# Where w_out's first half lands, and which engine issues the x tiles, in a pooling and gated-linear-attention block

## The chip, the cores and the metric

The kernel runs on one core of one Trainium2 chip. A core has a matrix engine (TensorE, PE in the profile; PEld is its weight load), a vector engine (VectorE, DVE), a scalar engine (ScalarE, ACT), GpSimd (POOL), and a sequencer (SyncE, SP) that in this kernel issues every transfer between memory and the core. Each engine works through its own list of instructions in order and waits for the others by semaphores. The metric is the device time of one execution in microseconds (us).

## What is computed

One block of a streaming encoder over 1024 rows of width 1024, after 16 meta rows: a mixer and a squared-ReLU MLP, all in float32. Cut to what matters here:

```python
def hybrid_mixer(u, ...):
    a, q, k, v, r, lr, ga, gb = split(u @ w_in)
    y_a = pooled(a) @ w_pool_out
    o = gla_chunked(q, k, v, log_a)                  # the attention, chunk by chunk
    y_b = (rmsnorm(o) * silu(r)) @ w_gla_out
    m = sigmoid(ga) * y_a + sigmoid(gb) * y_b        # the merge
    return m @ w_out
h = h + hybrid_mixer(rmsnorm(h), ...)
h = h + squared_relu_mlp(rmsnorm(h), w_ff1, w_ff2)
return rmsnorm(h)
```

The change sits between the end of `gla_chunked` and the product `m @ w_out`.

## The kernel before

**Split products.** Every float32 operand of a product is used as a high part (a copy rounded to the matrix engine's format, made by ACT) and a low part (the difference, made by DVE or POOL). A product is three matmuls for each 128 rows of depth, in `mm3` (L246 high by high, L247, L248). When the right-hand side is converted late, the first of the three needs only its high part, the second its low part. When the left-hand side is, the third needs its low part.

**Stages around the change.** The sequence is split into two halves of 512 rows. While the attention runs, a list of fill steps gives the matrix engine other work; the last of them are the merge blocks of half 0, `yb_block(n, 0)`. When the last attention unit has been started, `early_gates` runs: it turns on a hand-written order for ACT and DVE (their instructions then stand exactly in the order of the program text, as PE's do throughout), and takes space on the right-hand side of the memory for `t2`, `o2` and `raw3`, over tiles of the attention that are done (`n0`, `n1`, `f`, `y`, `lr`). Then come, in this order of the program: `merge_open`; the four merge blocks of half 1, `yb_block(0..3, 1)`; the conversion of the first half of w_out in four chunks of 512 KB, `load_wo(0, 0..3)`; `wo1_open`, which ends the hand-written order; eight output tiles `out_tile(t, 0)` for the left 512 columns, with the conversion of w_out's other half between them; eight output tiles for the right columns.

**A merge block** is two sub-blocks of 12 matmuls (four steps of depth by three). The text after the prediction's heading calls the blocks of half 1 B0 to B3, and their sub-blocks e0 and e1. DVE empties each sub-block's bank with L1060 (times a gate, `t`) and L1061 (plus the pooled part, `o`), ACT makes the high part (L1064, `th`), POOL the low part (L1065, `tl`). The gates and pooled parts are read back by SP (L1008, L1009) into three buffers each, so a load waits until POOL or DVE has used the buffer three sub-blocks earlier.

**w_gla_out** reaches the blocks through `W1`, a ring of two converted weights: SP loads into a raw tile (`Raw.load`, L101), ACT makes `w1h` (L77), DVE `w1l` (L78). B0 and B1 use weights kept from half 0. The weights of B2 are converted in the middle of B0 and those of B3 in the middle of B1, each between that block's two sub-blocks. Here they are called G2 and G3.

**w_out's chunks**, C0 to C3 here, are loaded into the same raw tiles and converted by ACT (L1345) and DVE (L1346). In the program text C0 stands behind B1, C1 behind B2, C2 and C3 behind B3. An output tile takes the four chunks one after the other, six matmuls each, and adds the x tile in L1378. The x tile was loaded into the same `acc` tile by SP (L1337, `x_again`), whose first tiles lie over buffers of the merge blocks of half 0.

**Banks.** Merge blocks and output tiles take turns over four banks of the matrix engine's result memory (`mm`, `mm`, `x`, `x`). Output tile 0 takes the bank that B2e0 had, so it cannot start before DVE has emptied that one.

**SP and POOL** are not in the hand-written order. The planner of the framework orders their instructions by its own estimate of when each becomes ready, and each then executes its list in that order.

Of the kernel before, what the change touches and what calls it, by code (L numbers as in the profile page):

```python
# [15 lines left out]
P = 128  # L16
D = 1024
# [3 lines left out]
HALF = 512  # L21
# [84 lines left out]
def kernel(  # L106
# [3 lines left out]
    nc = tc.nc  # L110
    x = x[0]
    out = out[0]
    norm_mix, w_in, w_pool_mix, pool_scale, w_pool_out = norm_mix[0], w_in[0], w_pool_mix[0], pool_scale[0], w_pool_out[0]
    w_gate_up, b_gate, gla_norm, w_gla_out, w_out = w_gate_up[0], b_gate[0], gla_norm[0], w_gla_out[0], w_out[0]
    norm_ffn, w_ff1, w_ff2 = norm_ffn[0], w_ff1[0], w_ff2[0]

    act, dve, pool, pe = nc.scalar, nc.vector, nc.gpsimd, nc.tensor
# [6 lines left out]
    def banks(keep=0, **tags):  # L124
        while len(ps_open) > keep:
            ps_open.pop().__exit__(None, None, None)
            wide.pop(psp.popitem()[0], None)
        for tag, n in tags.items():
            cm = tc.tile_pool(name=f"ps_{tag}", bufs=n, space=bass.MemoryType.PSUM)
            psp[tag] = cm.__enter__()  # L130
            ps_open.append(cm)
# [31 lines left out]
    gB = left.push("gB", [P, D], F32)  # L163
# [16 lines left out]
    raw = Raw(nc, [left.push(f"raw{i}", [P, D], F32) for i in range(2)])  # L180
# [10 lines left out]
    def f32(ap):  # L191
        return ap.bitcast(F32)
# [4 lines left out]
    def bcast(v):  # L197
        return v[None, :].broadcast_to([P, D])
# [202 lines left out]
    S, rings = {}, [W1]  # L401

    def step(steps, fn, ring=None, aps=()):
        steps.append((ring, list(aps), fn))
# [393 lines left out]
    one = []  # L798
# [122 lines left out]
    def rows4(w, j):  # L921
        return w[:, j * 256 : (j + 1) * 256].rearrange("(k p) c -> p k c", p=P)
# [79 lines left out]
    def yb_load(n, h):  # L1002

        if n >= 8 or (n, h) in staged:
            return
        d = 2 * YB[h][n // 2] + n % 2
        gl, ml = staged[n, h] = (nxt("t2"), nxt("o2")) if h else (nxt("t1"), nxt("o"))
        nc.sync.dma_start(gl, gb_dram[d, h])  # L1008
        nc.sync.dma_start(ml, ma_dram[d, h])  # L1009

    def in_order(on):


        if on:
            S["order"] = tc.manual_schedule(engines={mybir.EngineType.Activation, mybir.EngineType.DVE})
            S["order"].__enter__()
        else:
            S.pop("order").__exit__(None, None, None)

    def early_gates():  # L1020

        in_order(True)
        left.pop_to(S["left_n"])
        for key in ("t2", "o2"):
            S[key] = right.push(key, [P, 3, HALF], F32)
            S["n" + key], S["d" + key] = 0, 3
        S["raw3"] = right.push("raw3", [P, D], F32)
        for n in range(3):
            yb_load(n, 1)

# [2 lines left out]
    def yb_block(n, h):  # L1033
        j = YB[h][n]

        def fn(*wbs):
            if h == 0 and n > 1:
                kept[j] = wbs[0]
            wb = wbs[0] if wbs else kept[j]
            hi, lo = (t.rearrange("p (k c) -> p k c", k=4) for t in wb)  # L1040
            assert h or ("o", 0) in done
            yg = S["yg"][h]
            for e in range(2):
                d, w = 2 * j + e, slice(e * P, (e + 1) * P)
                for m in range(2 + h):
                    yb_load(2 * n + e + m, h)
                gl, ml = staged[2 * n + e, h]
                b = bank("mm")
                for k in range(4):
                    mm3(  # L1050
                        b, 1, lambda i: (hi[:, k, w], lo[:, k, w]),
                        lambda i: (yg[:, 0, k], yg[:, 1, k]), first=k == 0, last=k == 3,
                    )
                    yield 3 * 512 / 2400
                if e and not wbs:
                    W1.done, W1.kept = W1.done + 1, W1.kept - 1
                    W1.top_up()
                elif e:
                    yield "keep" if j in kept else "free"
                dve.tensor_tensor(gl, b, gl, ALU.mult)  # L1060
                dve.tensor_tensor(gl, gl, ml, ALU.add)  # L1061
                th = MH[h][:, d]
                tl = ML[h][:, d]
                act.activation(th, gl, ACT.Copy)  # L1064
                pool.tensor_tensor(tl, gl, f32(th), ALU.subtract)  # L1065

        return fn
# [216 lines left out]
    def gla():  # L1284
# [16 lines left out]
        for n, u in enumerate(units + [None]):  # L1301
            if u is None:
                early_gates()
            live = side + old + ([inside(*u, units[n - 1] if n else None)] if u else [])
            while live:
                waits = [(g, next(g, None)) for g in live]
                live = [g for g, w in waits if w is not None]
                pour(max([w for _, w in waits if w is not None], default=0) * PACE)
                if not live:
                    break  # L1310
            if n == 2:
                done.add(("o", 0))
            if n == 0:
                while ("k", 1) not in done:
                    next(filler)
            old = [across(*u)] if u else []
            side = [meta_state(1)] if n == 0 else []
# [7 lines left out]
    def merge_open():  # L1325
        W1.eng = dve
        banks(keep=1, x=2, ms=4)
        rota["mm"] = ("mm", "mm", "x", "x")
        left.pop_to(base)
        S["wo"] = [left.push("wo0", [P, 2, KT, HALF], F32R)]  # L1330
        S["left_acc"] = left.mark()
        S["acc"] = left.push("acc", [P, 8, D], F32)
        raw.lend(S["raw3"])
        nc.sync.dma_start(gB, bcast(norm_ffn))

    def x_again(t):
        nc.sync.dma_start(S["acc"][:, t], x[t * P : (t + 1) * P, :])  # L1337

    def load_wo(ch, kk):
        def fn():  # L1340
            wo = S["wo"][ch][:, :, 2 * kk : 2 * kk + 2]
            c = slice(ch * HALF, (ch + 1) * HALF)
            r = raw.load(w_out[kk * 256 : (kk + 1) * 256, c].rearrange("(k p) c -> p k c", p=P), D)
            r = r.rearrange("p (k c) -> p k c", k=2)
            act.activation(wo[:, 0], r, ACT.Copy)  # L1345
            dve.tensor_tensor(wo[:, 1], r, f32(wo[:, 0]), ALU.subtract)  # L1346

        return fn

    step(one, merge_open)  # L1350
    def wo1_open():
        in_order(False)
# [12 lines left out]
    def out_tile(t, ch):  # L1365
        def fn():
            half, at = t // 4, (t % 4) * P
            wo = S["wo"][ch]
            b, n = bank("mm"), ORDER.index(t)
            for j in range(2):  # L1370
                if ch and j and n > 1:
                    turn_tile(ORDER[n - 2])
                mm3(
                    b, KT // 2, lambda i: (MH[half][:, 4 * j + i, at : at + P], ML[half][:, 4 * j + i, at : at + P]),
                    lambda i: (wo[:, 0, 4 * j + i], wo[:, 1, 4 * j + i]), first=j == 0, last=j == 1,
                )
            a = S["acc"][:, t, ch * HALF : (ch + 1) * HALF]
            dve.tensor_tensor(a, b, a, ALU.add)  # L1378
            if ch:
                layer_norm(S["acc"][:, t], S["u2"][:, n % 2])  # L1380
                nc.sync.dma_start(h_dram[t], S["acc"][:, t])

        return fn

    def turn_tile(t, tags=("ms",)):
# [26 lines left out]
        for n, a in enumerate((lo, b12)):  # L1412
            fh, fl = (S["wo"][0][:, k, 4 * n : 4 * n + 4, cols] for k in range(2))
            act.activation(fh, a, ACT.Copy)
            dve.tensor_tensor(fl, a, f32(fh), ALU.subtract)

    for n, j in enumerate(YB[1]):
        if n < 2:
            step(one, yb_block(n, 1))
        else:  # L1420
            step(one, yb_block(n, 1), W1, [rows4(w_gla_out, j)])
        if n:
            step(one, load_wo(0, n - 1))
    step(one, load_wo(0, 3))
    step(one, wo1_open)
    for t in range(8):
        step(one, lambda t=t: x_again(t))
        step(one, out_tile(t, 0))
        if 1 < t < 6:
            step(one, load_wo(1, t - 2))  # L1430
# [268 lines left out]
```

## Time and profile before

| what | value |
|---|---|
| median of three runs | 1243.65 us (1243.61 to 1248.66) |
| the profiled execution | 1241.63 us, its span 1239.6 us |
| TensorE clock granted, mean | 0.996 of full |
| PE busy from 500 to 515 us | 15.00 of 15 us |
| PE busy from 515 to 525 us | 4.76 of 10 us |
| PE busy from 530 to 570 us | 40.00 of 40 us |

A row of the timeline gives the start in us, the length in us, engine, line, operation, the tile written and the tiles read, the number of instructions merged into the row, and in brackets how long the engine had been idle just before and what ended that. A row of the waits gives who waited for what, the total in us, how often, and the longest. A row of the windows gives, for a stretch of time, its length and the busy time of PE, PEld, DVE, ACT and POOL with instruction counts, then the granted clock, the share of the transfer engines' time in use, and GB/s. Successive matmuls of 512 columns start 0.23 us apart at full clock, though each is listed as 0.39 us long, since they are pipelined.

### The profile page before, as it was taken

Reading aid. Unit: us, or ns where it says so; the run is one execution under the profiler, and the core shown is the slowest. Engines: PE = TensorE matmul, PEld = TensorE weight load, DVE = VectorE, ACT = ScalarE, POOL = GpSimd, SP = SyncE. Lnnn points to the kernel's source line nnn. Section 1 sums busy time; section 2 is a strip of 40 time slices with the busy share of each in tenths; the row PEclk is TensorE's granted clock in tenths of the full one; section 3 lists DMA queues with packets and bytes.
Section 4 is the critical chain, followed back from the end, with each engine's and each line's share of the span. In section 5 each row is a group of like instructions: output and inputs, shape, how many; then the busy total and the mean of one; then the engine's idle time right before and its main releaser. Section 6 shows DMA issues by size and latency. Waiting matters only on the chain.

```text
span 1239.6 us, 18265 instructions
## 1 busy us (share of the span) xinstructions
PE 1206.1 (97%) x6816; PEld 1003.1 (81%) x6816; DVE 850.9 (69%) x1388; ACT 618.8 (50%) x1099; POOL 66.6 (5%) x74
## 2 busy tenths in 40 slices
PE   7999999999999999899999999999999999999997
PEld 6878888988887778688878888888887788888886
DVE  6896676654556676634896676776774877887686
ACT  6667567322446663412654454555553444444554
POOL 2100000001101015400000000000000000000000
PEclk9999999999999999899999999999999999999999
DMA  8033326146102247831244444444569863333432
GB/s 250 2 110 104 110 86 193 53 155 219 36 19 78 69 133 234 282 109 51 98 125 159 156 153 143 162 156 134 176 216 374 289 235 102 94 99 98 162 98 89
DMA packets 142680, 173.84 MB, mean 140 GB/s; under 512 B 10968, under 2 KB 82416, under 8 KB 142592
## 3 DMA queue, kind: packets, MB, share of 16 engines
q1 hardware_dynamic: 142592, 172.68, 43.3%
q8 instruction: 53, 0.87, 0.3%
q14 instruction: 35, 0.29, 0.1%
HBM read 119.17 MB, written 53.48 MB: 139 GB/s over the span
## 4 chain that ended last, share of the span: by engine, by line
PE 85%; DVE 8%; ACT 3%; DMA 2%; issue 2%; SPq 0%; DVEq 0%; ACTq 0%
PE b_mm L246 10%; PE b_mm L247 10%; PE b_mm L248 10%; PE b_ms L247 9%; PE b_ms L246 9%; PE b_ms L248 9%; PE b_x L248 8%; PE b_x L246 8%; PE b_x L247 8%; PE b_sc L1147 1%; PE b_ms L550 1%; PE b_mx L246 1%; PE b_m L1249 1%; PE b_mx L247 1%; PE b_mx L248 1%
## 5 line engine op out<-in xcount | busy, mean ns | idle before, releaser
L246 PE MATMUL b_mm<-th,w1h 128*128 128x512 f32 (+1 forms) x312 | 117.6, 377 | 1.9 <-DVE c L761 1.1
L247 PE MATMUL b_mm<-tl,w1h 128*128 128x512 f32 (+1 forms) x312 | 116.0, 372 | 0.6 <-DVE tl L1407 0.6
L248 PE MATMUL b_mm<-th,w1l 128*128 128x512 f32 (+1 forms) x312 | 115.8, 371 | 0.0
L246 PE MATMUL b_x<-th,w1h 128*128 128x512 f32 (+1 forms) x240 | 90.8, 378 | 0.0
L247 PE MATMUL b_x<-tl,w1h 128*128 128x512 f32 (+1 forms) x240 | 90.6, 378 | 0.0
L248 PE MATMUL b_x<-th,w1l 128*128 128x512 f32 (+1 forms) x240 | 90.3, 376 | 0.0
L264 ACT ACTIVATE w1h<-raw 128x512 fp32r<-128x512 f32 x96 | 59.6, 621 | 36.8 <-PE b_x L247 14.1
L265 DVE TENSOR_TENSOR w1l<-raw,w1h 128x512 fp32r<-128x512 f32 x96 | 65.6, 684 | 12.9 <-ACT w1h L264 12.9
L246 PEld LDWEIGHTS b_mm<-th,w1h 128*128 128x128 f32 x312 | 58.6, 188 | 13.7 <-issue 1.8
L264 ACT ACTIVATE w1h<-fs 128x512 fp32r<-128x512 f32 x72 | 45.4, 631 | 45.8 <-PE b_ms L247 31.5
L247 PEld LDWEIGHTS b_mm<-tl,w1h 128*128 128x128 f32 x312 | 58.6, 188 | 10.6 <-DVE tl L1407 0.9
L248 PEld LDWEIGHTS b_mm<-th,w1l 128*128 128x128 f32 x312 | 58.6, 188 | 10.3
L264 ACT ACTIVATE w1h<-bt 128x512 fp32r<-128x512 f32 x44 | 27.8, 632 | 67.7 <-issue 59.6
L265 DVE TENSOR_TENSOR w1l<-fs,w1h 128x512 fp32r<-128x512 f32 x72 | 49.3, 685 | 14.7 <-ACT w1h L264 14.6
L1556 DVE TENSOR_TENSOR bt<-w,w 128x512 f32<-128x512 f32 x80 | 54.6, 683 | 1.0 <-DMA w<-in_w_ff_dram 1.0
L248 PEld LDWEIGHTS b_x<-th,w1l 128*128 128x128 f32 x240 | 45.1, 188 | 8.4
L246 PEld LDWEIGHTS b_x<-th,w1h 128*128 128x128 f32 x240 | 45.0, 188 | 8.5
L247 PEld LDWEIGHTS b_x<-tl,w1h 128*128 128x128 f32 x240 | 45.1, 188 | 8.3
L264 ACT ACTIVATE fxh<-bt 128x512 fp32r<-128x512 f32 x36 | 22.8, 632 | 55.4 <-issue 48.1
L246 PE MATMUL b_ms<-wo,w1h 128*128 128x512 f32 x128 | 49.8, 389 | 0.0
L247 PE MATMUL b_ms<-wo,w1h 128*128 128x512 f32 x128 | 49.8, 389 | 0.0
L248 PE MATMUL b_ms<-wo,w1l 128*128 128x512 f32 x128 | 49.8, 389 | 0.0
(446 smaller groups left out, 3365.2 us busy)
## 6 DMA issues: line engine op xcount, KB each, us to landing
hf_dram<-h SPq DMA_DIRECT2D x112, 256.0 KB, 2.1
raw<-hf_dram SPq DMA_DIRECT2D x112, 256.0 KB, 2.7
w<-in_w_ff_dram SPq DMA_DIRECT2D x64, 256.0 KB, 4.9
raw<-in_w_in_dram SPq DMA_DIRECT2D x24, 512.0 KB, 4.9
raw<-in_w_ff_dram SPq DMA_DIRECT2D x16, 512.0 KB, 4.1
rawx<-in_w_ff_dram SPq DMA_DIRECT2D x16, 512.0 KB, 4.1
xs<-in_x_dram SPq DMA_DIRECT2D x8, 512.0 KB, 4.7
rawx<-in_w_in_dram SPq DMA_DIRECT2D x8, 512.0 KB, 4.7
```

The source lines that it names most:

```text
L246: pe.matmul(ps, ah, bh, start=first and i == 0, stop=False, skip_group_check=more)
L247: pe.matmul(ps, ah, bl, start=False, stop=False, skip_group_check=more)
L248: pe.matmul(ps, al, bh, start=False, stop=last and i == n - 1, skip_group_check=more)
L264: act.activation(hi, a, ACT.Copy)
L265: dve.tensor_tensor(lo, a, f32(hi), ALU.subtract)
L550: pe.transpose(b[j][:, i], u[:, (4 * j + i) * P : (4 * j + i + 1) * P], ident)
L1147: pe.matmul(b[to, e, j], kk[r, s], qq[r, s], start=True, stop=True, tile_position=(e * CH, u * CH))
L1249: pe.matmul(o[part(u), e, j], scc[part(u), e, j], v[part(u), j, e], start=j == 0, stop=False, tile_position=(u * CH, u * CH), skip_group_c ...
L1556: dve.tensor_tensor(bt, w, S["w2"][q[3:]][:, i], ALU.add if q[2] == "+" else ALU.subtract)
```

## The change

C0 is loaded into `raw3` already in `early_gates`, and `raw3` is no longer one of the raw tiles. C1, C2 and C3 are loaded into the last three tiles of `acc` as soon as `merge_open` has made them. The conversions of C0, C1 and C2 move forward by two blocks and that of C3 by one: C0 stands ahead of B0, C1 ahead of B1, C2 ahead of B2, C3 ahead of B3. The x tiles and the row `gB` are issued by ACT in place of SP: tile 0 before B3, tile 1 after B3, tile t + 2 ahead of output tile t. SP is not put into a hand-written order.

```diff
@@ early_gates
         S["raw3"] = right.push("raw3", [P, D], F32)
+        fetch_wo(0, 0, S["raw3"])
         for n in range(3):
             yb_load(n, 1)
@@ merge_open and behind it
         S["acc"] = left.push("acc", [P, 8, D], F32)
-        raw.lend(S["raw3"])
-        nc.sync.dma_start(gB, bcast(norm_ffn))
+        for kk in (1, 2, 3):
+            fetch_wo(0, kk, S["acc"][:, 4 + kk])
+
+    def load_gB():
+        act.dma_start(gB, bcast(norm_ffn))
 
     def x_again(t):
-        nc.sync.dma_start(S["acc"][:, t], x[t * P : (t + 1) * P, :])
+        act.dma_start(S["acc"][:, t], x[t * P : (t + 1) * P, :])
+
+    fetched = {}
+
+    def fetch_wo(ch, kk, at=None):
+
+        c, rows = slice(ch * HALF, (ch + 1) * HALF), w_out[kk * 256 : (kk + 1) * 256]
+        ap = rows[:, c].rearrange("(k p) c -> p k c", p=P)
+        if at is None:
+            at = raw.load(ap, D)
+        else:
+            nc.sync.dma_start(at.rearrange("p (k c) -> p k c", k=2), ap)
+        fetched[ch, kk] = at.rearrange("p (k c) -> p k c", k=2)
 
     def load_wo(ch, kk):
         def fn():
-            wo = S["wo"][ch][:, :, 2 * kk : 2 * kk + 2]
-            c = slice(ch * HALF, (ch + 1) * HALF)
-            r = raw.load(w_out[kk * 256 : (kk + 1) * 256, c].rearrange("(k p) c -> p k c", p=P), D)
-            r = r.rearrange("p (k c) -> p k c", k=2)
+            if (ch, kk) not in fetched:
+                fetch_wo(ch, kk)
+            wo, r = S["wo"][ch][:, :, 2 * kk : 2 * kk + 2], fetched.pop((ch, kk))
             act.activation(wo[:, 0], r, ACT.Copy)
             dve.tensor_tensor(wo[:, 1], r, f32(wo[:, 0]), ALU.subtract)
@@ the list of steps
+    def loads(*ts):
+        def fn():
+            for t in ts:
+                x_again(t)
+
+        return fn
+
     for n, j in enumerate(YB[1]):
+        step(one, load_wo(0, n))
+        if n == 3:
+            step(one, loads(0))
         if n < 2:
             step(one, yb_block(n, 1))
         else:
             step(one, yb_block(n, 1), W1, [rows4(w_gla_out, j)])
-        if n:
-            step(one, load_wo(0, n - 1))
-    step(one, load_wo(0, 3))
+    step(one, loads(1))
     step(one, wo1_open)
+    step(one, lambda: load_gB())
     for t in range(8):
-        step(one, lambda t=t: x_again(t))
+        if t < 6:
+            step(one, loads(t + 2))
         step(one, out_tile(t, 0))
         if 1 < t < 6:
             step(one, load_wo(1, t - 2))
```

## The prediction

> **What bounds the kernel now.** I read the page's first rows, then the matrix engine's waits, longest first, to find a hole that this change could close.
>
> ```profile
> span 1239.6 us, 18265 instructions
> PE 1206.1 (97%) x6816; PEld 1003.1 (81%) x6816; DVE 850.9 (69%) x1388; ACT 618.8 (50%) x1099; POOL 66.6 (5%) x74
> ```
>
> ```profile
> PE b_mm L246 <- ACT wo L1345: 2.8, 1, 2.8
> PE b_mm L247 <- DVE wo L1346: 2.4, 2, 1.4
> ```
>
> PE sets the time: it is busy for 97% of the span. Its two longest waits in the middle of the kernel are both for w_out's chunks. Its timeline shows where.
>
> ```profile
> 513.66 0.39 PE L246 MATMUL b_mm<-wo,th 128*128 128x512 f32 x1
> ...
> 516.99 0.50 PE L247 MATMUL b_mm<-wo,th 128*128 128x512 f32 x1 [1.37 <-DVE wo L1346]
> ...
> 521.25 0.79 PE L246 MATMUL b_mm<-wo,th 128*128 128x512 f32 x1 [2.83 <-ACT wo L1345]
> 523.09 0.80 PE L247 MATMUL b_mm<-wo,th 128*128 128x512 f32 x1 [1.04 <-DVE wo L1346]
> ...
> 527.09 0.39 PE L246 MATMUL b_x<-wo,th 128*128 128x512 f32 x1
> ```
>
> Output tile 0 starts at 513.66 and tile 1 at 527.09: 13.43 us for 24 matmuls. Part of that is a lower clock, as the windows of one microsecond show (the last column but two).
>
> ```profile
> 519.00:520.00 1.00, 0.00 (x0) 0.00 (x0) 0.59 (x1) 0.38 (x1) 1.00 (x1) 0.62 0.85 164
> 520.00:521.00 1.00, 0.00 (x0) 0.00 (x0) 0.00 (x0) 1.00 (x2) 1.00 (x2) 0.50 0.88 225
> ...
> 526.00:527.00 1.00, 1.00 (x6) 0.82 (x5) 1.00 (x2) 0.22 (x1) 0.00 (x0) 0.97 0.97 348
> ```
>
> The pace without a hole is read from the block before it.
>
> ```profile
> 503.24 0.39 PE L248 MATMUL b_mm<-yg,w1l 128*128 128x512 f32 x1
> ...
> 508.22 0.39 PE L246 MATMUL b_x<-yg,w1h 128*128 128x512 f32 x1
> 508.45 0.39 PE L247 MATMUL b_x<-yg,w1h 128*128 128x512 f32 x1
> 508.68 0.39 PE L248 MATMUL b_x<-yg,w1l 128*128 128x512 f32 x1
> ```
>
> B3 runs from 508.22 to 513.66: 24 matmuls in 5.44 us, or 0.227 each. So the hole costs 13.43 - 5.44 = 7.99 us. That is all the change can win: PE is full from 530 to 570.
>
> Why the chunks are late is read from DVE, ACT and POOL, whose order is fixed by hand for the first two.
>
> ```profile
> 494.32 0.69 DVE L1061 TENSOR_TENSOR t<-t,o 128x512 f32<-128x512 f32 x1
> 494.93 0.69 DVE L1060 TENSOR_TENSOR t<-b_mm,t 128x512 f32<-128x512 f32 x1
> ...
> 498.46 1.75 DVE L78 TENSOR_TENSOR w1l<-raw,w1h 128x1024 fp32r<-128x1024 f32 x1 [1.74 <-ACT w1h L77]
> ...
> 504.51 1.85 DVE L78 TENSOR_TENSOR w1l<-raw,w1h 128x1024 fp32r<-128x1024 f32 x1 [1.65 <-ACT w1h L77]
> ...
> 512.76 0.69 DVE L1061 TENSOR_TENSOR t<-t,o 128x512 f32<-128x512 f32 x1
> 515.10 1.83 DVE L1346 TENSOR_TENSOR wo<-raw,wo 128x1024 fp32r<-128x1024 f32 x1 [1.65 <-ACT wo L1345]
> 516.86 0.68 DVE L1060 TENSOR_TENSOR t<-b_x,t 128x512 f32<-128x512 f32 x1
> ...
> 521.23 2.94 DVE L1346 TENSOR_TENSOR wo<-raw,wo 128x1024 fp32r<-128x1024 f32 x2 [1.64 <-DMA raw<-in_w_out_dram]
> ```
>
> ```profile
> 495.05 0.64 ACT L1064 ACTIVATE th<-t 128x512 fp32r<-128x512 f32 x1 [0.70 <-DVE t L1061]
> ...
> 497.36 1.06 ACT L77 ACTIVATE w1h<-raw 128x1024 fp32r<-128x1024 f32 x1
> ...
> 508.25 1.04 ACT L1345 ACTIVATE wo<-raw 128x1024 fp32r<-128x1024 f32 x1
> ...
> 520.16 1.99 ACT L1345 ACTIVATE wo<-raw 128x1024 fp32r<-128x1024 f32 x2
> ```
>
> ```profile
> 494.43 4.70 POOL L1065 TENSOR_TENSOR tl<-t,th 128x512 fp32r<-128x512 f32 x3 [3.15 <-ACT th L1064]
> ...
> 502.28 3.00 POOL L1065 TENSOR_TENSOR tl<-t,th 128x512 fp32r<-128x512 f32 x2 [3.15 <-ACT th L1064]
> ```
>
> From 494.93 on, DVE and ACT hand the work to each other and each waits for the other. C2's high part starts at 520.16 because ACT had nothing to start it with earlier in its order, not because C2 was late in landing. So the bound is this **serial chain**, not a transfer. One chunk put between two sub-blocks costs the chain 516.86 - (512.76 + 0.69) = 3.41 us: the wait for `th`, ACT's copy, DVE's difference.
>
> **The change, part by part.** The chain begins again where half 0 ends, DVE at 494.32 + 0.69 = 495.01, ACT at 495.69. Durations are those of the rows: L1060 0.72 and L1061 0.61 to 0.72 from start to start, `th` 0.64 with ACT free again after 0.53, a high part 1.05. A low part made while POOL works ends 1.08 us after POOL (498.46 + 1.75 = 500.21 against 494.43 + 4.70 = 499.13; 504.51 + 1.85 = 506.36 against 505.28). With POOL working in one of its operations of 1.3 to 1.5 us, that makes some 1.5 us, as it starts 0.9 after the POOL operation does.
>
> C0 ahead of B0: ACT 495.6 to 496.65, DVE from 496.7. POOL ends the second of its three operations at about 494.43 + 2/3 x 4.70 = 497.6, taken as 497.4 as the first is shorter, so C0 is done at 498.5. B0e0 starts on DVE at 498.4 instead of 494.93.
>
> G2: B0e0 ends 499.85, `th`, ACT copies w1h 500.4 to 501.45, DVE ends w1l at 503.0. PE reads it in the third matmul of B2 at 503.24: in time, by 0.2.
>
> C1 ahead of B1: B0e1 on DVE to 504.3, `th` 504.35, ACT's copy 504.9 to 505.95, difference to 507.5. B1e0 on DVE to 508.85.
>
> G3, behind it: `th` 508.85, copy 509.4 to 510.45, difference to 512.0. **Here the stall goes.** PE wants w1h of B3 at 508.22 and w1l at 508.68. It starts B3 at 510.45, does two matmuls, and waits again until 512.05: 3.37 us lost in two holes of 2.2 and 1.1 us. Before, w1l was done at 506.36, 2.3 us early; two chunks ahead of it cost more. B3's other 22 matmuls end at 512.05 + 22 x 0.227 = 517.05.
>
> C2, C3: B1e1 512.0 to 513.4, C2 513.9 to 516.5, B2 to 519.1, C3's copy 519.75 to 520.8, difference to 522.4. Output tile 0 starts at 517.15 (its bank is read by B2e0's L1060 from 516.45), does 18 matmuls to 521.25, one more, waits 0.9 for C3's low part, and does the last 5 by 522.4 + 5 x 0.227 = 523.55. Against 527.09 that is a **gain of 3.5 us** at full clock.
>
> **The clock** in the new holes is not shown by the trace of before. From below it costs nothing, for which there is a nearby row with PE busy 1.16 of 2 us and the clock at 1.00:
>
> ```profile
> 78.00:80.00 2.00, 1.16 (x6) 0.59 (x4) 2.00 (x4) 0.00 (x0) 0.00 (x0) 1.00 1.04 295
> ```
>
> From above, half clock from 519.3 to 526 came after 1.4 us of work between holes of 1.37 and 2.83; 6.7 us of it from 512 would cost 3.4 us on PE, less the 0.9 that PE waits for C3 anyway: 2.5. The new holes have even less work between them (0.45 us) but sum to 3.3 us instead of 4.2 before the drop; I take 0.8, a third. The sum is -3.5 + 0.8 = **-2.7 us**. The Trainium skill ("TensorE: Matmul & The Clock Gate", "Why this matters for your kernels") says that the clock holds as long as no idle gap is longer than about 3 us. By that rule the holes would cost no clock and the gain would be 3.5; but no gap here was longer than 2.83 and the clock fell all the same, so the row decides.
>
> **What I cost at nothing.** The transfers and who issues them, by the windows, the timeline, the issues (size, median us to landing) and SP's waits:
>
> ```profile
> 492.00:495.00 3.00, 3.00 (x15) 2.49 (x14) 2.93 (x6) 0.63 (x1) 0.57 (x1) 1.00 0.04 15
> 495.00:498.00 3.00, 3.00 (x15) 2.48 (x14) 1.69 (x3) 1.88 (x3) 3.00 (x3) 1.00 0.00 0
> ```
>
> ```profile
> 491.12 1.24 DVE L1281 TENSOR_TENSOR yg<-mix,yg 128x1024 fp32r<-128x1024 f32 x1 [1.13 <-ACT yg L1280]
> ```
>
> ```profile
> 497.90 0.33 SPq L1337 DMA_DIRECT2D acc<-in_x_dram  x1
> ```
>
> ```profile
> acc<-in_x_dram SPq DMA_DIRECT2D x8, 512.0 KB, 6.6
> ...
> raw<-in_w_out_dram SPq DMA_DIRECT2D x7, 512.0 KB, 6.2
> ```
>
> ```profile
> SPq L1337 <- POOL tl L1065: 5.1, 1, 5.1
> ...
> SPq L1337 <- DMA t<-gb_dram: 2.2, 1, 2.2
> ```
>
> C0 goes out once `n0` is free and lands some 6.2 us later; C0 is wanted at 495.6, well after the attention's inner part has ended. C1 to C3 lie over `mix`, last read by L1281 to 492.4, at the latest where `acc`'s first load went, 497.9. The transfer engines are empty then (0.04 and 0.00). With 6.2 us C1 lands between 498.6 and 504.1, wanted at 504.9: **in time by 0.8 to 6.3**; without that cover each us late is about one us of time. G3's raw tile, now one of two, is free long before (ACT copies it at 509.4). On ACT stand nine new issues. No row shows one on ACT; SP's takes 0.33 us, and the bounds are 0 and the 2.2 us that one waited on SP for a transfer of another tile. Queued behind x0 on ACT are `th` of B3e0 and POOL's low part, which output tile 4 reads first, four tiles of 5.44 us after tile 0; behind x1 the conversions of w_out's other half, wanted a round later. So 0, even at 2.2. An x tile lands 6.6 us after its issue, x0 at 527.4; the add in L1378 then holds one of four banks, wanted again 16 us later. `gB` is first read in the second round. SP loses nine issues that nobody waited for.
>
> **The rivals.**
>
> *The hole closes.* If G3 were done by 508.68 in spite of the order and the chunks ahead of tile 0, all 7.99 us would be won: 1243.65 - 8.0 = 1235.7. For it: the chunks do land and convert earlier, ACT idles between its rows. Against it: the chain is serial, and two chunks at 3 us and more stand ahead of a conversion that had 2.3 us to spare.
>
> *C1 comes late and the kernel is slower.* SP waits in order, and its planner may put C1 behind a load of `t` that waits for POOL. It can stand as late as behind the fifth, whose buffer POOL gives back after B0e1, at about 506.5 in the new order. Then C1 lands at 506.5 + 6.2 = 512.7, 7.8 late. G3, C2 and C3 move with it, output tile 0 ends at 531.3, and a hole of ten us costs some 1.7 us more at half clock: 6.0 us slower, 1249.6. It decides from 3.5 us late (C1 after 508.4), where the gain is gone. For it: the waits of 5.1 and 2.2 us on SP. Against it: C1 stands earlier in the program than those loads.
>
> *It is given back.* The chain's sum is the same work in another order; if the cold clock takes its full 2.5 and C1 is a little late, nothing is left: 1243.5.
>
> **How the numbers follow.** The chain as worked out 0.50, the closed hole 0.20, late C1 0.20, given back 0.10. The profiled execution would go from 1241.63 to 1238.9; it stands 2.0 below the median of the three runs, so the median goes from 1243.65 to 1240.9. The likeliest case's own range is 1239.5 (no cold clock, a little better packing) to 1243. The range takes in the closed hole at 1235.7 and most of the late C1, to 1248. Half a per cent is 6.2 us, about what a measurement of this kernel can tell from no change: faster by that needs 1237.4, which is the closed hole and the best edge of the chain, 0.24; slower, 1249.9, is the worse part of the late C1 and what I have not seen, 0.16; within it 0.60.
>
> **What would show it.** Right: in the new profile PE waits for `w1h` and `w1l` at the head of B3, some 2 and 1 us, then for C3's low part under 1 us, and not for C1 or C2; DVE's L1346 of C0 stands before B0's L1060; the third matmul of B3 comes some 3.4 us later than before and output tile 1 starts some 3 us earlier. Wrong: PE runs through B3, or ACT's L1345 waits for a transfer, or a wait on ACT behind an x issue reaches PE.

## The result, and the profile after

| | before | after |
|---|---|---|
| median, eight runs each | 1245.80 us (1243.61 to 1249.42) | 1240.49 us (1238.41 to 1242.68) |
| ratio, 95% interval | | 0.9961 [0.9949, 0.9973] |
| profiled execution; span | 1241.63; 1239.6 us | 1239.61; 1237.8 us |

By the ratio the kernel is 0.39% faster, which is 4.9 us of the 1243.65 that the prediction started from, with an interval of 3.4 to 6.3 us (the two medians of the table lie 5.3 apart). That is inside the half per cent that the prediction called no change. The forecast was a time of 1240.9, close to the measured one, and a gain of 2.7 us, which is less than the measured gain and below its interval.

The first rows of the page of the kernel after: the span, and each engine's busy time.

```profile
span 1237.8 us, 18267 instructions
PE 1206.8 (97%) x6816; PEld 1004.8 (81%) x6816; DVE 850.8 (69%) x1388; ACT 618.4 (50%) x1099; POOL 65.9 (5%) x74
```

The engines do the same work as before. What changed is where PE stands idle. These are its waits from 495 to 530 us after the change (who waited for what, the total in us, how often, the longest).

```profile
PE b_x L246 <- ACT w1h L77: 2.0, 1, 2.0
PE b_mm L247 <- DVE wo L1361: 0.9, 1, 0.9
PE b_x L248 <- DVE w1l L78: 0.7, 1, 0.7
```

Of the waits for w_out before, 2.8 and 2.4 us, only 0.9 is left. Two new waits for the weight of block B3 stand in their place. (L1360 and L1361 after the change are L1345 and L1346 before it; L1061, L1062 and L1065 are L1060, L1061 and L1064.) The timeline of PE in the kernel after shows where.

```profile
504.30 0.39 PE L246 MATMUL b_mm<-yg,w1h 128*128 128x512 f32 x1
...
511.90 0.50 PE L246 MATMUL b_x<-yg,w1h 128*128 128x512 f32 x1 [2.00 <-ACT w1h L77]
512.24 0.40 PE L247 MATMUL b_x<-yg,w1h 128*128 128x512 f32 x1
513.38 0.50 PE L248 MATMUL b_x<-yg,w1l 128*128 128x512 f32 x1 [0.75 <-DVE w1l L78]
...
518.50 0.42 PE L246 MATMUL b_mm<-wo,th 128*128 128x512 f32 x1
...
523.97 0.50 PE L247 MATMUL b_mm<-wo,th 128*128 128x512 f32 x1 [0.93 <-DVE wo L1361]
...
525.24 0.40 PE L246 MATMUL b_x<-wo,th 128*128 128x512 f32 x1
```

The rows are the first matmul of B2, the three first of B3, the first of output tile 0, the late one in tile 0, and the first of tile 1. From B2's first to tile 1's first lie 72 matmuls, 16.32 us at 0.227 each. What the stage takes beyond that is called **the hole** from here on: 525.24 - 504.30 - 16.32 = 4.62 us. Before it was 7.99. The stage gives 3.37 us.

The span shrank by less, 1.8 us, because this execution was late already when it came to the stage: half 0 ends on DVE (the first row below) at 495.84, where the execution before had 494.32, 1.52 us earlier; 3.37 - 1.52 is 1.85. Most of that, 1.25 us, was there more than 400 us earlier, where the change does nothing. Here is the same matmul on PE's timeline, of the kernel before and of the kernel after.

```profile
76.57 0.51 PE L248 MATMUL b_ms<-P4h,w1l 128*128 128x512 f32 x1 [1.78 <-DVE w1l L265]
```

```profile
77.82 0.53 PE L248 MATMUL b_ms<-P4h,w1l 128*128 128x512 f32 x1 [1.80 <-DVE w1l L265]
```

So stages are compared below by their holes, and whole kernels by ratios over many runs.

The chain itself, DVE's timeline in the kernel after:

```profile
495.84 0.69 DVE L1062 TENSOR_TENSOR t<-t,o 128x512 f32<-128x512 f32 x1
498.18 1.84 DVE L1361 TENSOR_TENSOR wo<-raw,wo 128x1024 fp32r<-128x1024 f32 x1 [1.65 <-ACT wo L1360]
...
503.05 1.42 DVE L78 TENSOR_TENSOR w1l<-raw,w1h 128x1024 fp32r<-128x1024 f32 x1 [1.71 <-ACT w1h L77]
...
507.50 1.41 DVE L1361 TENSOR_TENSOR wo<-acc,wo 128x1024 fp32r<-128x1024 f32 x1 [1.71 <-ACT wo L1360]
...
511.88 1.45 DVE L78 TENSOR_TENSOR w1l<-raw,w1h 128x1024 fp32r<-128x1024 f32 x1 [1.64 <-ACT w1h L77]
513.25 0.68 DVE L1061 TENSOR_TENSOR t<-b_mm,t 128x512 f32<-128x512 f32 x1
...
516.30 1.47 DVE L1361 TENSOR_TENSOR wo<-acc,wo 128x1024 fp32r<-128x1024 f32 x1 [1.65 <-ACT wo L1360]
...
522.08 1.84 DVE L1361 TENSOR_TENSOR wo<-acc,wo 128x1024 fp32r<-128x1024 f32 x1 [1.65 <-ACT wo L1360]
```

Read downward this is C0, G2, C1, G3, B1e1's first operation, C2, C3. Each low part waits for ACT's copy (the brackets), and none for a transfer. Two chunks stand ahead of G3, whose low part ends at 513.33; PE ran out of B2 near 509.9.

ACT and SP in the kernel after: the copy of C0, the first x tiles, the high part of B0e0; and the three transfers of C1 to C3.

```profile
497.10 1.05 ACT L1360 ACTIVATE wo<-raw 128x1024 fp32r<-128x1024 f32 x1
498.97 0.92 ACTq L1341 DMA_DIRECT2D acc<-in_x_dram  x2
501.38 0.63 ACT L1065 ACTIVATE th<-t 128x512 fp32r<-128x512 f32 x1 [3.23 <-DVE t L1062]
```

```profile
498.97 1.41 SPq L1352 DMA_DIRECT2D acc<-in_w_out_dram  x3
```

The program text puts x0 before B3. ACT issues it, with the next one, before B0's first high part, at the moment at which SP issues C1 to C3. ACT's issues do not keep the place that its hand-written order gives to its copies. The prediction had taken them to stand in that order. Here the early issue cost nothing on ACT: it had finished the copy of C0 at 498.15, and B0e0's `t` was ready only at 501.34.

### The profile page after: what moved, and what is told of

The parts are those of the page before. It is cut to its first block, busy times and chain, and to the rows that moved or that the text cites. A ratio compares the mean times of both kernels' runs of the same rounds, so it can differ in the third digit from the quotient of the medians.

```text
span 1237.8 us, 18267 instructions
## 1 busy us (share of the span) xinstructions
PE 1206.8 (97%) x6816; PEld 1004.8 (81%) x6816; DVE 850.8 (69%) x1388; ACT 618.4 (50%) x1099; POOL 65.9 (5%) x74
## 4 chain that ended last, share of the span: by engine, by line
PE 86%; DVE 8%; ACT 3%; issue 2%; DMA 2%; SPq 0%; DVEq 0%; ACTq 0%
PE b_mm L246 10%; PE b_mm L247 10%; PE b_mm L248 10%; PE b_ms L248 9%; PE b_ms L246 9%; PE b_ms L247 9%; PE b_x L248 8%; PE b_x L246 8%; PE b_x L247 8%; PE b_sc L1148 1%; PE b_ms L550 1%; PE b_mx L246 1%; PE b_m L1250 1%; PE b_mx L248 1%; PE b_mx L247 1%
## 5 line engine op out<-in xcount | busy, mean ns | idle before, releaser
L247 PEld LDWEIGHTS b_mm<-tl,w1h 128*128 128x128 f32 x312 | 58.7, 188 | 10.7 <-DVE tl L1422 0.9
## 6 DMA issues: line engine op xcount, KB each, us to landing
raw<-in_w_in_dram SPq DMA_DIRECT2D x24, 512.0 KB, 4.5
raw<-in_w_ff_dram SPq DMA_DIRECT2D x16, 512.0 KB, 4.2
rawx<-in_w_ff_dram SPq DMA_DIRECT2D x16, 512.0 KB, 4.1
xs<-in_x_dram SPq DMA_DIRECT2D x8, 512.0 KB, 4.8
rawx<-in_w_in_dram SPq DMA_DIRECT2D x8, 512.0 KB, 4.7
```

What stands on the lines that cost most here:

```text
L247: pe.matmul(ps, ah, bl, start=False, stop=False, skip_group_check=more)
```

## The experiments

"The theory" below is the prediction's: the gain and the new loss both come from the order of conversions in the chain of DVE and ACT, not from where the chunks land or who issues the x tiles. All ratios are to the kernel before, measured beside each kernel on the same chip. The hole is read as above, in the profiled execution. At full clock each wait of PE leaves a hole 0.3 to 0.4 us longer than itself until the pace is back: in the kernel after, three waits of 3.68 us in all make a hole of 4.62. What a kernel saves of the hole of 7.99 and what it saves by the ratio differ by up to 1.5 us, and the ratios of neighbouring rows often overlap, so fine steps below rest on the hole of one execution each.

| kernel | hole, us | median, us | ratio [95%] |
|---|---|---|---|
| after | 4.62 | 1240.49 | 0.9961 [0.9949, 0.9973] |
| order only | 4.62 | 1240.02 | 0.9968 [0.9957, 0.9980] |
| places and x on ACT, old order | 14.03 | 1249.39 | 1.0039 [1.0027, 1.0051] |
| places, x on SP, old order | 8.23 | 1244.21 | 1.0004 [0.9994, 1.0015] |
| after, x on SP | 4.62 | 1240.18 | 0.9975 [0.9966, 0.9983] |
| C1 behind B1 | 4.67 | 1240.95 | 0.9972 [0.9961, 0.9983] |
| C1 behind B1, x on SP | 3.03 | 1238.27 | 0.9957 [0.9944, 0.9971] |
| all chunks behind G3 | 2.58 | 1237.18 | 0.9948 [0.9936, 0.9960] |
| all chunks behind G3, x on SP | 0.00 | 1234.14 | 0.9925 [0.9912, 0.9938] |
| before, chunks behind G3 | 1.17 | 1235.45 | 0.9937 [0.9925, 0.9949] |

### The order alone

The kernel before, with only the conversions in the order of the change; chunks still land in the raw tiles, and SP issues the x tiles.

```diff
     for n, j in enumerate(YB[1]):
+        step(one, load_wo(0, n))
         ...
-        if n:
-            step(one, load_wo(0, n - 1))
-    step(one, load_wo(0, 3))
```

> The kernel before with nothing changed but the place of the conversions in the order (C0 ahead of B0, C1 ahead of B1, C2 ahead of B2, C3 ahead of B3); the loads stay in the raw tiles and the x tiles on SP. Measure: the time from B2's first matmul to output tile 1's first, less 72 matmuls at 0.227 us; 8.0 us before, 4.6 with the change. Chain theory: the raw tiles come free early enough (C0's long before, C1's with G2's weights of the half before, C2's after G2, C3's after C1), so the hole is 4.6 +- 0.7 and the time 3.4 us under before, ratio 0.997. Rival, the idle tiles bring the gain: hole 7 or more, time as before.

PE's timeline in this kernel:

```profile
510.96 0.50 PE L246 MATMUL b_x<-yg,w1h 128*128 128x512 f32 x1 [2.00 <-ACT w1h L77]
...
512.45 0.50 PE L248 MATMUL b_x<-yg,w1l 128*128 128x512 f32 x1 [0.75 <-DVE w1l L78]
...
523.04 0.50 PE L247 MATMUL b_mm<-wo,th 128*128 128x512 f32 x1 [0.93 <-DVE wo L1346]
```

The three waits are those of the changed kernel to the hundredth, and so is the hole, 4.62. The order of conversions, the part of the change that the title does not name, alone makes its whole effect on this stage.

### The places, without the order

The changed kernel with the conversions put back to where they were before: the chunks land early in idle tiles, and ACT issues the x tiles.

```diff
     for n, j in enumerate(YB[1]):
-        step(one, load_wo(0, n))
         ...
+        if n:
+            step(one, load_wo(0, n - 1))
+    step(one, load_wo(0, 3))
```

> The changed kernel with the conversions put back where they stood (C0 behind B1, C1 behind B2, C2 and C3 behind B3); w_out still lands in the idle tiles and ACT still issues the x tiles. Chain theory: hole 8.0 +- 0.7 as before, ratio 1.000 (0.998 to 1.002). Rival, the idle tiles or the issuing engine bring the gain: hole 4.6, ratio 0.997.

This missed on both sides: the hole grew by 6.04 us to 14.03 and the kernel became slower by 0.27 to 0.51%. PE waited for a bank twice (0.72 and 1.56 us) and for w_out four times (1.95, 1.33, 3.37 and 0.69). What was late is seen on DVE, then on ACT and SP, all of this kernel.

```profile
511.04 0.69 DVE L1061 TENSOR_TENSOR t<-b_mm,t 128x512 f32<-128x512 f32 x1 [3.51 <-DMA t<-gb_dram]
```

```profile
497.86 0.40 ACTq L1341 DMA_DIRECT2D acc<-in_x_dram  x1
498.30 0.63 ACT L1065 ACTIVATE th<-t 128x512 fp32r<-128x512 f32 x1 [2.67 <-POOL tl L1066]
498.35 0.94 ACTq L1341 DMA_DIRECT2D acc<-in_x_dram  x2
```

```profile
497.86 1.41 SPq L1352 DMA_DIRECT2D acc<-in_w_out_dram  x3
500.33 0.34 SPq L1008 DMA_DIRECT2D t<-gb_dram  x1
```

Two things are read here. DVE stood 3.51 us for the gate tile of B1e1, issued at 500.33 and used at 511.04, 10.7 us later: six transfers of 512 KB (three chunks, three x tiles) had been issued ahead of it. And B0e0's high part on ACT waited 2.67 us for POOL: x0's tile lies over a buffer that POOL was still reading, and the issue of x0 held ACT until then. G2's low part began at 499.97 for that, against 498.45 with SP issuing. To tell the places from the issuing engine, the next two kernels have SP issue the x tiles and `gB`.

### The x tiles issued by SP

One is the kernel just shown, the other the changed kernel, each with this edit:

```diff
     def load_gB():
-        act.dma_start(gB, bcast(norm_ffn))
+        nc.sync.dma_start(gB, bcast(norm_ffn))

     def x_again(t):
-        act.dma_start(S["acc"][:, t], x[t * P : (t + 1) * P, :])
+        nc.sync.dma_start(S["acc"][:, t], x[t * P : (t + 1) * P, :])
```

In the old order:

> The kernel with the changed landing places but the conversions where they stood (hole 14.0, not the 8.0 expected), now with the x tiles issued by SP. Theory: there three chunks of w_out and three x tiles, 3 MB, went out in the same microsecond ahead of the fourth gate tile, which landed 10 us after its issue, and the issue of x tile 0 held ACT 2.7 us until POOL was done; half of the 3 MB and the hold on ACT are the x tiles'. So hole 8 to 10, ratio 1.000 to 1.002. Rival, the chunks alone do it: hole 12 or more, ratio 1.003 or more.

The hole is 8.23 with waits of 1.36, 2.83 and 1.04, those of the kernel before; the ratio is 1.0004. So early landing alone is worth nothing in the old order, and the 5.8 us between 14.03 and 8.23 are the issue of the x tiles and `gB` on ACT. B1e1's first operation on DVE, in this kernel:

```profile
506.40 0.69 DVE L1061 TENSOR_TENSOR t<-b_mm,t 128x512 f32<-128x512 f32 x1
```

With x on ACT it came at 511.04, 4.64 us later, and the wait that ended last there was that for the gate tile (3.51 us). The hold on ACT had a part in it: the load of that tile was issued at 500.33, right after POOL had given its buffer back at 500.30, against 499.34 here.

In the order of the change:

> The changed kernel with the x tiles and gB issued by SP again, everything else as changed. Theory: in the changed order DVE takes the fourth gate tile at 513, so late that nobody waits for the transfers that the x tiles hold up; hole 4.6 +- 0.5 and ratio 0.997 as with the change. Rival, ACT as issuer is a part of the gain: hole 5.5 or more.

The hole is 4.62 again, with waits of 2.00, 0.75 and 0.95. The same issues that cost 5.8 us in the old order cost nothing here, because the new order is late by itself: B1e1's first operation stands at 513.25 on DVE in the changed kernel (quoted above), behind C0, C1 and G3, and finds its gate tile there. ACT's hold and the crowded transfers were not tried apart; an estimate from the times above gives the hold about 1 of the 4.64 us by which B1e1 was late, and the transfers the rest.

### One chunk less ahead of G3

The changed kernel with C1 converted behind B1, together with C2.

```diff
-        step(one, load_wo(0, n))
+        for kk in {0: (0,), 2: (1, 2), 3: (3,)}.get(n, ()):
+            step(one, load_wo(0, kk))
```

> The changed kernel with C1 moved from ahead of B1 to ahead of C2 and B2, so that one chunk in place of two stands ahead of G3. Chain theory: w1l of B3 is done at 508.7 on the scale of before, when PE wants it, so B3 runs through; output tile 0 waits 1.4 us for its bank (B2e0's L1060 stands behind two chunks now) and 1 us for C3: hole 2.4 us, 5.6 us under before, ratio 0.9955. Rival, the hole at B3 has another cause than the chunks ahead of G3: B3 still waits 3 us, hole 5 or more.

Here half came as expected. B3 ran through but for 0.32 us of wait, so the slope is right: two chunks ahead of G3 make B3's third matmul some 3.2 us late, one makes it 0.5 late (0.3 of wait and the return to pace). But the hole stayed at 4.67. On DVE and then on PE of this kernel:

```profile
511.09 0.69 DVE L1061 TENSOR_TENSOR t<-b_mm,t 128x512 f32<-128x512 f32 x1 [1.15 <-DMA t<-gb_dram]
```

```profile
517.45 0.69 PE L246 MATMUL b_mm<-wo,th 128*128 128x512 f32 x1 [2.16 <-DVE t L1061]
```

With the chain sooner, the gate tile was the late one, by 1.15 us, and output tile 0 waited 2.16 us for its bank. Behind that wait the clock fell, as the windows of one microsecond of this kernel show (length, busy PE, PEld, DVE, ACT, POOL, then the granted clock, transfer share and GB/s).

```profile
517.00:518.00 1.00, 0.55 (x2) 0.46 (x3) 0.96 (x2) 0.00 (x0) 0.00 (x0) 0.80 0.90 281
518.00:519.00 1.00, 1.00 (x4) 0.81 (x3) 0.96 (x3) 0.63 (x1) 0.14 (x1) 0.50 0.99 289
...
520.00:521.00 1.00, 1.00 (x4) 0.75 (x3) 0.00 (x0) 1.00 (x2) 1.00 (x2) 0.50 1.01 414
```

With SP issuing the x tiles and `gB` (the edit above) on top of this one:

> C1 behind B1 (hole 4.7 with ACT issuing the x tiles, 2.4 expected), now with the x tiles issued by SP. Theory: what was missing in that sum was the gate tile that lands late (DVE waited 1.2 us for it) and the clock that fell behind the longer wait; without the x tiles ahead of it the sum holds: output tile 0 waits 1.0 to 1.5 us for its bank and 0.5 to 1 us for C3, hole 2.4 +- 0.6, ratio 0.9945 to 0.9960. Rival, the sum misses something in the chain itself: hole 4 or more.

The hole is 3.03, just outside what was expected (1.8 to 3.0): PE waited 0.32 for `w1l`, 0.90 for the bank and 0.90 for C3's low part, and the return to pace after the three waits makes up the rest. DVE did not wait for B1e1's gate tile, and the clock stayed at 1.00.

### All chunks behind G3

If two chunks ahead of G3 cost 3 us, none should cost nothing. ACT's four copies are put behind that of G3 and ahead of B1e1's high part; DVE makes the low parts in two pairs, ahead of B2 and between its two sub-blocks.

```diff
@@ the second pass of a merge block, ahead of DVE's two operations
+                if (h, n, e) == (1, 1, 1):
+                    highs(0, 1, 2, 3)
+                if (h, n, e) == (1, 2, 1):
+                    lows(2, 3)()
@@ the list of steps
-        step(one, load_wo(0, n))
+        if n == 2:
+            step(one, lows(0, 1))
```

`highs` makes the copies of the chunks it is given, `lows` returns a step that makes their differences. First with the x tiles on ACT:

> The changed kernel with no chunk ahead of G3: ACT makes the four high parts right behind w1h of B3, DVE the low parts of C0 and C1 behind B1 and those of C2 and C3 between the two sub-blocks of B2. Chain theory: G3 done as early as before the change, all chunks done by 515 to 517 while PE wants them from 513.7 to 518: hole 0 to 0.7 us, 8 us under before, ratio 0.9936. Rival, transfers: C1 to C3 are issued at 498 and land too late for an ACT that wants them at 506 to 509, th of B1e1 and the conversions wait, and the hole is 3 us or more.

The hole is 2.58, less than in any kernel so far and more than expected; PE waits 0.24 and 1.80 us for a bank. DVE's timeline of this kernel again has the gate tile of B1e1:

```profile
511.26 0.69 DVE L1065 TENSOR_TENSOR t<-b_mm,t 128x512 f32<-128x512 f32 x1 [3.02 <-DMA t<-gb_dram]
```

Then with the x tiles and `gB` on SP:

> The order with all conversions behind G3 (hole 2.6 with ACT issuing the x tiles), now with the x tiles issued by SP behind the gate loads. Theory: DVE's wait of 3.0 us for the fourth gate tile goes to 1 or less and ACT's of 2.7 for POOL is gone, hole 0 to 1, ratio 0.993. Rival, the chunks alone hold up the gate tile: hole stays at 2 or more, ratio 0.995.

The same operation in this kernel, and the windows of five microseconds of the stage:

```profile
507.85 0.69 DVE L1065 TENSOR_TENSOR t<-b_mm,t 128x512 f32<-128x512 f32 x1 [0.28 <-DMA t<-gb_dram]
```

```profile
505.00:510.00 5.00, 5.00 (x24) 4.14 (x23) 3.96 (x4) 5.00 (x6) 1.48 (x2) 1.00 0.88 285
510.00:515.00 5.00, 5.00 (x24) 4.14 (x23) 4.96 (x5) 0.63 (x1) 1.77 (x2) 1.00 0.92 321
515.00:520.00 5.00, 5.00 (x24) 4.14 (x23) 4.91 (x6) 0.63 (x1) 1.85 (x2) 1.00 0.97 304
520.00:525.00 5.00, 5.00 (x24) 4.14 (x23) 3.13 (x3) 1.27 (x2) 3.67 (x3) 1.00 0.91 291
```

PE is busy for 5.00 of 5.00 us in every window: the hole is closed. At 0.9925 this kernel beats both the kernel before and the change, and the intervals do not touch. It differs from the one before it only in who issues the x tiles and `gB`. In the stretch from 497 to 512 us a load of a gate tile takes 4.3 us to land in this kernel, 7.9 in the one before it and 8.1 in the old-order kernel with x on ACT, in the median; the issues of the first and the last of these (KB each, median us to landing):

```profile
acc<-in_w_out_dram SPq DMA_DIRECT2D x3, 512.0 KB, 4.4
t<-gb_dram SPq DMA_DIRECT2D x4, 256.0 KB, 4.3
```

```profile
acc<-in_w_out_dram SPq DMA_DIRECT2D x3, 512.0 KB, 8.6
acc<-in_x_dram ACTq DMA_DIRECT2D x3, 512.0 KB, 9.0
...
t<-gb_dram SPq DMA_DIRECT2D x3, 256.0 KB, 8.1
```

### The same without the idle tiles

The kernel before, with the conversions behind G3, chunks still loaded into the raw tiles (by `highs`, ahead of each copy) and x on SP: the copies of C0 and C1 ahead of DVE's work on B1e1, those of C2 and C3 on B2e0, the differences as above.

```diff
+                if (h, n, e) == (1, 1, 1):
+                    highs(0, 1)
+                if (h, n, e) == (1, 2, 0):
+                    highs(2, 3)
+                if (h, n, e) == (1, 2, 1):
+                    lows(2, 3)()
@@ the list of steps
+        if n == 2:
+            step(one, lows(0, 1))
-        if n:
-            step(one, load_wo(0, n - 1))
-    step(one, load_wo(0, 3))
```

> The kernel before (raw tiles, x by SP) with the conversions behind G3: ACT makes the high parts of C0 and C1 behind w1h of B3 and those of C2 and C3 behind B2's first sub-block, DVE the low parts of C0 and C1 behind B1, of C2 and C3 inside B2. Theory: the raw tiles give C1 back after G2 (500), C2 after G3 (506), C3 after C0 (509), landing some 6 us later, each just in time: hole 0 to 2, ratio 0.993 to 0.995, so the idle tiles are not needed. Rival, the raw tiles come free too late: ACT waits for C2 or C3 and the hole is 4 or more.

The hole is 1.17: PE waits once, 0.75 us for a low part of w_out. Now a transfer is late, on ACT, whose waits from 490 to 530 us have this row:

```profile
ACT wo L1351 <- DMA raw<-in_w_out_dram: 8.4, 3, 3.6
```

Only with the order right does the place of landing show, in the 1.2 us between this hole and the closed one (medians 1235.45 and 1234.14; the intervals of the two ratios overlap). C3's copy waited 3.6 us for its transfer, and its low part is what PE waited for. The copies of C2 and C3 also stand later here, so it is not shown that all of the 1.2 us is the place's.

## Why the prediction was right, and where its steps were not

The chain held step by step. The times after are set back by the 1.52 us that the execution was late.

| step of the prediction | forecast | after, set back |
|---|---|---|
| C0's low part done | 498.5 | 498.50 |
| G2's low part done | 503.0 | 502.95 |
| C1's low part done | 507.5 | 507.39 |
| G3's low part done | 512.0 | 511.81 |
| B3's third matmul | 512.05 | 511.86 |
| output tile 0 starts | 517.15 | 516.98 |
| C3's low part done | 522.4 | 522.40 |
| output tile 1 starts | 523.55 | 523.72 |

**Gain at full clock.** The prediction's signs of being right came about: set back, the third matmul of B3 stands 3.2 us later than before (3.4 forecast), tile 1 starts 3.37 us earlier, and PE does not wait for C1 or C2. Forecast 3.5, in the trace 3.37. The kernel with the order alone shows that it is the order's: the same hole, a ratio of 0.9968. The measured gain of the median, 3.4 to 6.3 us, holds 3.37 only just; the kernels with the same stage gave 2.5 to 5.4 (order only) and 2.1 to 4.2 us (x on SP). What the median gained beyond 3.37 is not explained. That the time came within 0.4 us of the forecast is partly luck: a gain forecast too small was taken off 1243.65, the median of three runs, where eight runs gave 1245.80.

**Where the stall goes.** The two holes at the head of B3, forecast at 2.2 and 1.1 us from start to start, were 2.15 and 1.03 so counted (waits of 2.00 and 0.75). The hole for C3's low part, forecast 0.9, was 1.16 (a wait of 0.93). B2 was in time, by 0.3 us.

**The clock.** This term was mis-sized: I took 0.8 us, between 0 and 2.5, and it was 0, as in the other two kernels with these waits (order only; x on SP). The comparison behind it was also misread. Before the change the clock did not fall after 4.2 us of holes: the mean of 0.62 from 519 to 520 puts the fall at about 519.2, when the hole of 2.83 us, which began at 518.42, was 0.8 us old. So 2.2 us of idle stood ahead of that drop, less than the 2.75 us of waits after the change. The windows of one microsecond of the kernel after, across the two holes, have the clock in the last column but two.

```profile
510.00:511.00 1.00, 0.00 (x0) 0.00 (x0) 0.24 (x1) 0.73 (x2) 0.02 (x1) 1.00 1.06 391
511.00:512.00 1.00, 0.10 (x1) 0.10 (x1) 0.12 (x1) 0.85 (x1) 1.00 (x1) 1.00 1.05 379
512.00:513.00 1.00, 0.64 (x2) 0.20 (x2) 1.00 (x1) 0.00 (x0) 0.25 (x1) 1.00 1.06 401
513.00:514.00 1.00, 0.62 (x3) 0.53 (x4) 0.97 (x3) 0.00 (x0) 0.00 (x0) 1.00 1.03 399
```

The rule of the Trainium skill that the prediction weighed ("TensorE: Matmul & The Clock Gate", "Why this matters for your kernels": to avoid drops, no idle gap of more than about 3 us) would have given the better sum here, with gaps of 2.00 and 0.75 at 1.00. It fails in the kernel with C1 behind B1, where one gap of 2.16 was followed by 0.50.

**What was costed at nothing.** Landing in idle tiles: right, 8.23 against 7.99 and no wait for C1 or C2. The nine issues on ACT: the sum was right, the reason wrong. The prediction placed x0 before B3, with `th` of B3e0 queued behind it and nothing that mattered before output tile 4, and bounded its wait at 2.2 us. Its own rows held the warning, which it did not use: x0's issue on SP had waited 5.1 us for POOL, and in the old order with x on ACT the same wait held `th` of B0e0 for 2.67. x0 went out before B0's `th`, beside C1 to C3, and in an order with an earlier chain it cost 5.8 us of hole (14.03 against 8.23), 2.58 (against 0.00) or 1.64 (4.67 against 3.03, where the lower clock has a part in it). The change's own late chain hid that price.

**The rivals.** *The hole closes* did not come about, for the reason given against it; it needed the order with no chunk ahead of G3, and then gave 1234.14 against the 1235.7 worked out. *C1 comes late*: SP issued C1 at 498.97, and ACT copied it with no wait for a transfer. The delay of a later load was real all the same, by another way: not C1 behind a gate's load, but the gate's load behind the chunks and x tiles, in the kernels with a sooner chain. *Given back*: the clock did not fall.

## What to carry to other kernels

Where two engines hand work to each other in a fixed order, put the conversion that is wanted first ahead of those wanted later, and count each one inserted by what it delays: here the order alone was worth 3.4 us of the hole as the change had it and 6.8 with nothing ahead of the urgent conversion, while early landing was worth nothing in the old order and at most 1.2 with the conversions behind G3. Before moving DMA issues to another engine, look where they come out in the trace, what their target still waits for, and which small load follows them: the price may be hidden by a lateness that the next improvement takes away.

## What the runs showed of the hardware that was not expected

The length of an idle gap did not settle what the clock did. The matmul near 77 us that was quoted above waited 1.78 us in the kernel before and 1.80 in the kernel after, in code that is the same. The prediction quoted the window that followed before the change, 78 to 80 us at a clock of 1.00; here is the same window after it.

```profile
78.00:80.00 2.00, 2.00 (x6) 1.57 (x7) 2.00 (x4) 0.00 (x0) 0.00 (x0) 0.54 0.79 120
```

Near half clock after the one, full clock after the other (before the change, every window of one microsecond from 75 to 84 us shows 1.00); likewise gaps of 2.00 and 0.75 us at 1.00 in the changed kernel, and a drop for some 3 us behind 2.16 us in the kernel with C1 behind B1. Nine matmuls there took 3.74 us (517.45 to 521.19) in place of 2.04, so such a drop costs PE about 1.7 us. Little of that reached the stage: C3's low part was done only at 522.91, and at full clock PE would have wanted it at 521.76 (19 matmuls at 0.227 after 517.45). What decides between drop and no drop was not settled.

A DMA issue on ACT whose target tile was still being read held ACT's computation as well: `th` stood 2.67 us in the old-order kernel behind an issue for another tile.
